# One 512-column matmul for the high and low part of the input, and two weight sums formed by accumulating DMAs

## The chip, the cores and the metric

One NeuronCore of a Trainium2 chip. The metric is device time of one launch in microseconds, the median of several runs. The engines are PE (matrix), DVE (vector), ACT (scalar), POOL and SP; SP and ACT start plain DMAs here, and POOL starts none in the kernel before.

## The reference

A decoder block over 512 positions of width 2048, all float32: an input projection, two kinds of mixer heads, an output projection, and then a gated feed-forward part, which the change touches:

```
h = rms_norm(x, norm2) * (1 + sc2) + sh2
gate, val = split(h @ w_up, 2)              # w_up: 2048 x 12288, two halves of 6144
gate = causal_dwconv(gate, ffn_conv_w, ffn_conv_b)     # three taps along the sequence
x = x + g2 * ((gelu(gate) * val) @ w_down)  # w_down: 6144 x 2048
out = rms_norm(x, norm_final)
```

`sh2, sc2, g2` come from `silu(c) @ w_ada`, a conditioning product of a vector and a large matrix.

## The kernel before

**Precision.** Every operand of a large matmul is kept as two tiles of a rounded matmul type: a high part (the value rounded) and a low part (what rounding left off). A product is three matmuls: high weights by high input, high weights by low input, low weights by high input. For weights, ACT rounds a raw block (`round_up`, L162) and DVE subtracts (`rest`, L167).

**Steps.** The work is a list of steps, each with one weight block of 128 x 1024 numbers and 24 matmuls. The main loop issues, for step j: what is put at j with half -1; the rounding of the weights of step j+2; the fetch of raw weights for j+5; what is put at j with half 0; the remainder of the weights of j+2; the first half of the matmuls; what is put with half 1; the second half. Each engine works through its own instructions in that order, so `put(j, fn, cost, half)` decides where a small piece of work stands in DVE's, ACT's, SP's or POOL's queue. Buffers come from pools with a fixed number per tag; a tile waits until the last user of its buffer is done.

**The up projection.** The first four columns of 128 features (steps UP0 to UP0+15) are plain: 512-column matmuls over 16 blocks of the input. For the other 44 columns, gate, value, the two halves of the positions and the two halves of the 2048 inputs make a 2 x 2 by 2 x 2 block product, which is done with seven products instead of eight (`P1` to `P7`, `product`, L859). For each product a step multiplies a sum of weight blocks by a sum of input blocks; 8 blocks of 128 inputs, 256 positions, three matmuls of 256 columns each (L875 to L877). Every product uses only the first half (`lower`) of a PSUM bank. The steps of a column go P1, then P4 and P3 of the column before, then P2, P6, P5, P7.

`combine` (L820) forms the four sums of input blocks (DVE), rounds them (ACT) and takes the remainders (DVE), one portion k of eight per plain step from UP0+8 on. `column` (L896) does the rest for a column: four weight blocks are loaded on SP (`split_load`), DVE forms four sums of them (t1 to t4), ACT copies P1, P6, P7 and P4 out of PSUM (`after_p1` and so on), DVE adds P2, P7 and P3 to those copies, then the convolution taps, gelu, the product of gate and value, and a store to DRAM (`act_kept`) on SP.

**The down projection** (steps from J1 on) loads these activations again (`act_load`, L1044), splits them (`act_split`, L1048) and multiplies by w_down with 512-column matmuls, in two halves of 24 activations, four groups of 12 steps each. After a group, `settle` (L978) adds the group's banks to the residual with a factor g2, whose 16 columns come from `g2_load` (1 MB of w_ada into one buffer) and `ada` (a product on DVE, L209), put at J1+4 to J1+35. There are six banks for groups, and a group takes four.

Of the kernel before, what the change touches and what calls it, by code (L numbers as in the profile page):

```python
# [50 lines left out]
def tile_block(ctx, tc, x_t, vec, w_ada, w_in, w_r, w_i, ws_t, w_out, w_up, w_us, w_dn, out):  # L51
# [144 lines left out]
    def ada_load(n, pl=mid):  # L196
        w = D + (2 if n // KT in (1, 4) else 1)
        loads[0] += 1
        front = pl is mid and early_open and loads[0] % 3 == 0
        if front:  # L200
            raw = sb("araw2", 1, (P, D + 2), pl=fore)
        else:
            raw = sb("araw", 2 if pl is mid else 1, (P, D + (2 if pl is mid else 32)), pl=pl)
        SY.dma_start(raw[:, :w], w_ada[n, :, :w])
        return n, raw[:, :w], w, front

# [613 lines left out]
    def combine(k):  # L820

        a, b = x2[k], x2[k + KT // 2]
        sh, shb = (mod(3 * KT + n) for n in (k, k + KT // 2))
        st = sb("rawb", 4, (P, 4, HS), pl=ffn)
        V.scalar_tensor_tensor(out=st[:, 1, :], in0=a[:, upper], scalar=shsum[:, k:k + 1], in1=b[:, upper],
                               op0=ADD, op1=ADD)
        V.scalar_tensor_tensor(out=st[:, 0, :], in0=st[:, 1, :], scalar=sh, in1=a[:, lower], op0=SUB, op1=SUB)
        V.tensor_tensor(out=st[:, 2, :], in0=a[:, upper], in1=a[:, lower], op=SUB)
        V.scalar_tensor_tensor(out=st[:, 3, :], in0=b[:, lower], scalar=shb, in1=st[:, 0, :], op0=ADD, op1=SUB)
        sums[k] = []  # L830
        for i in range(4):
            two = sb("sx", 8, (P, 2, HS), F32R, ffn) if k in (2, 3) else sb("xs", NXS, (P, 2, HS), F32R)
            A.copy(two[:, 0, :], st[:, i, :])
            sums[k].append(two)

        def rest():
            for i in range(4):
                V.tensor_tensor(out=sums[k][i][:, 1, :], in0=st[:, i, :], in1=sums[k][i][:, 0, :], op=SUB)
        return rest

    def combine_all():
        V.tensor_tensor(out=shsum, in0=mods[:, 3 * KT:3 * KT + KT // 2], in1=mods[:, 3 * KT + KT // 2:4 * KT], op=ADD)
# [16 lines left out]
    def product(f, p):  # L859
        j = len(steps)  # L860
        place[p, f] = j
        b = INTO[p]
        source[j] = lambda: of[f][p]

        def go(kk):
            if p in ("P1", "P2", "P5") and kk == 0:
                of[f][b] = bank()
            ps = of[f][b][:, lower]
            hi, lo = ws[j][kk]
            for k in range(4 * kk, 4 * kk + 4):  # L870
# [18 lines left out]
            product(n, p)  # L889

    def split_load(f, i, tag):
        t = sb("raw", 4, (P, 2, S)) if tag == "raw" else sb("rawb", 4, (P, 2, S), pl=ffn)
        SY.dma_start(t, w_us[f - PLAIN, i])
        return t

    def column(f):  # L896
        o = of[f]
        at_ = {p: place[p, f] for p in INTO}
        s = at_["P1"]

        def load(name, i, tag):
            o[name] = split_load(f, i, tag)

        put(s - 6, lambda: load("P1", 0, "raw"), 0.0, 1)
        put(s - 5, lambda: load("b12", 1, "raw"), 0.0, 1)
        put(s - 4, lambda: load("P3", 3, "rawb"), 0.0, 1)
        put(s - 3, lambda: load("P2", 2, "rawb"), 0.0, 1)

        def t1():
            V.tensor_tensor(out=o["P1"], in0=o["b12"], in1=o["P1"], op=SUB)  # L910
            o["P5"] = o["P1"]

        def t2():
            o["P6"] = sb("t2", 1, (P, 2, S), pl=ffn)
            V.tensor_tensor(out=o["P6"], in0=o["P3"], in1=o["P5"], op=SUB)

        def t3():
            V.tensor_tensor(out=o["b12"], in0=o["b12"], in1=o["P3"], op=SUB)
            o["P7"] = o["b12"]

        def t4():
            V.tensor_tensor(out=o["P2"], in0=o["P2"], in1=o["P6"], op=SUB)
# [6 lines left out]
        def half(tag):  # L929
            return sb(tag, 1, (P, HS), pl=ffn)  # L930

        def after_p1():
            o["c1"] = half("c1")
            A.copy(o["c1"], o["x"][:, lower])

        def after_p2():
            o["g"] = sb("fg", 2, pl=ffn)
            V.tensor_tensor(out=o["g"][:, lower], in0=o["z"][:, lower], in1=o["c1"], op=ADD)

        def after_p6():  # L940
            o["u2"] = half("u2")
            A.copy(o["u2"], o["x"][:, lower])

        def after_p7():
            u3 = half("u3")
            A.copy(u3, o["x"][:, lower])
            o["v"] = sb("fv", 2, pl=ffn)
            V.tensor_tensor(out=o["v"][:, upper], in0=o["y"][:, lower], in1=u3, op=ADD)

        def after_p4():  # L950
            A.copy(o["g"][:, upper], o["x"][:, lower])
# [3 lines left out]
        def after_p3():  # L955
            V.tensor_tensor(out=o["v"][:, lower], in0=o["y"][:, lower], in1=o["u2"], op=ADD)

        def times():
            V.tensor_tensor(out=o["fy"], in0=o["fy"], in1=o["v"], op=MUL)
# [7 lines left out]
        put(at_["P3"] + 2, lambda: tap(f, o["fy"], o["g"], 1))  # L967
# [23 lines left out]

    def weigh(n, apart=False):

        q = sb("yl", 3, pl=room2[0]) if n else xs()
        A.activation(q, x2[n], AF.Square)  # L995
        w = sb("yl", 3, pl=room2[0]) if apart else x2[n]
        V.tensor_scalar(out=w, in0=x2[n], scalar1=gfh[:, n:n + 1], scalar2=None, op0=MUL)
        x2[n] = w
        if n:
            V.tensor_tensor(out=total[0], in0=total[0], in1=q, op=ADD)  # L1000
        else:
            total[0] = q
# [37 lines left out]
                group_by_column(srcs, ks, act, down_tail, 2)  # L1040

    yls = {}

    def act_load(f):  # L1044
        yls[f] = sb("yl", 3, pl=room2[0] or ffn)
        SY.dma_start(yls[f], kept[f])

    def act_split(f):  # L1048
        y = yls.pop(f)
        two = pair() if f < 16 or 27 <= f < 43 else sb("dp", 11, (P, 2, S), F32R, room2[0])  # L1050
        A.copy(two[:, 0, :], y)
        V.tensor_tensor(out=two[:, 1, :], in0=y, in1=two[:, 0, :], op=SUB)
        act[f] = (two[:, 0, :], two[:, 1, :], two)

    def second_room():
        opened.pop().__exit__(None, None, None)
# [154 lines left out]
```

## Time and profile before

| | us |
|---|---|
| median of 3 runs | 2150.6 (2147.19 to 2150.71) |
| the profiled execution | 2149.32 |
| its span, first to last instruction | 2147.6 |
| mean granted clock of the matrix engine | 0.989 of 2.4 GHz |

The span is what the trace's times count from; 1.7 us of the execution lie around it. A timeline row is a start, a duration, the engine, the source line, the operation and its tiles; in brackets stand the idle time before it and what ended that. Durations of matmuls overlap, so starts are compared.

### The profile page before, as it was taken

Reading aid. Unit: us, or ns where it says so; the run is one execution under the profiler, and the core shown is the slowest. Engines: PE = TensorE matmul, PEld = TensorE weight load, DVE = VectorE, ACT = ScalarE, POOL = GpSimd, SP = SyncE. Lnnn points to the kernel's source line nnn. Section 1 sums busy time; section 2 is a strip of 40 time slices with the busy share of each in tenths; the row PEclk is TensorE's granted clock in tenths of the full one; section 3 lists DMA queues with packets and bytes.
Section 4 is the critical chain, followed back from the end, with each engine's and each line's share of the span. In section 5 each row is a group of like instructions: output and inputs, shape, how many; then the busy total and the mean of one; then the engine's idle time right before and its main releaser. Section 6 shows DMA issues by size and latency. Waiting matters only on the chain. (4 is left out here: it accounts for less than half of the span.)

```text
span 2147.6 us, 30757 instructions
## 1 busy us (share of the span) xinstructions
PE 2094.9 (98%) x12620; PEld 1861.4 (87%) x12620; DVE 1508.0 (70%) x1851; ACT 875.0 (41%) x1148; POOL 4.7 (0%) x12
## 2 busy tenths in 40 slices
PE   7999999999989999999999999999998999999996
PEld 4887778888768999999999999999997888888885
DVE  8999889787768777877877877877865444432333
ACT  5323775332234544544544444444452112222222
POOL 0000000000000000000000000000000000000000
PEclk8999999999999999999999999999999999999998
DMA  9876443679822333233233233233256555422222
GB/s 369 331 286 222 147 157 129 225 285 336 301 96 99 126 131 131 93 132 128 94 133 127 95 133 127 95 133 127 96 182 258 217 210 182 160 91 98 89 98 79
DMA packets 97069, 351.43 MB, mean 164 GB/s; under 512 B 12704, under 2 KB 12832, under 8 KB 84640
## 3 DMA queue, kind: packets, MB, share of 16 engines
q1 hardware_dynamic: 81520, 293.36, 38.3%
q10 hardware_dynamic: 15408, 56.11, 7.2%
q8 instruction: 99, 1.62, 0.3%
q14 instruction: 42, 0.34, 0.0%
HBM read 328.45 MB, written 20.97 MB: 163 GB/s over the span
## 5 line engine op out<-in xcount | busy, mean ns | idle before, releaser
L162 ACT CAST wh<-raw 128x1024 fp32r<-128x1024 f32 x340 | 356.9, 1050 | 694.4 <-PE mm L174 483.8
L167 DVE TENSOR_TENSOR wl<-raw,wh 128x1024 fp32r<-128x1024 f32 x340 | 416.0, 1224 | 238.4 <-ACT wh L162 235.8
L173 PE MATMUL mm<-hp,wh 128*128 128x512 f32 x1280 | 508.7, 397 | 15.2 <-DVE xs L979 5.8
L175 PE MATMUL mm<-hp,wl 128*128 128x512 f32 x1280 | 502.2, 392 | 3.1 <-DVE wl L167 3.1
L174 PE MATMUL mm<-hp,wh 128*128 128x512 f32 x1280 | 502.5, 393 | 0.8 <-DVE hp L234 0.8
L173 PEld LDWEIGHTS mm<-hp,wh 128*128 128x128 f32 x1280 | 242.7, 190 | 72.4 <-ACT hp L226 9.1
L877 PE MATMUL mm<-xs,wl 128*128 128x256 f32 x1056 | 299.1, 283 | 0.6 <-DVE wl L167 0.5
L875 PE MATMUL mm<-xs,wh 128*128 128x256 f32 x1056 | 298.9, 283 | 0.0
L876 PE MATMUL mm<-hp,wh 128*128 128x256 f32 x1056 | 298.9, 283 | 0.0
L877 PE MATMUL mm<-hp,wl 128*128 128x256 f32 x1056 | 298.8, 283 | 0.0
L875 PE MATMUL mm<-hp,wh 128*128 128x256 f32 x1056 | 298.8, 283 | 0.0
L876 PE MATMUL mm<-xs,wh 128*128 128x256 f32 x1056 | 298.8, 283 | 0.0
L175 PEld LDWEIGHTS mm<-hp,wl 128*128 128x128 f32 x1280 | 242.5, 189 | 55.1 <-DVE wl L167 4.4
L174 PEld LDWEIGHTS mm<-hp,wh 128*128 128x128 f32 x1280 | 242.5, 189 | 54.3 <-issue 2.4
L209 DVE SCALAR_TENSOR_TENSOR araw<-araw,crow 128x2050 f32<-128x2050 f32 (+1 forms) x96 | 219.8, 2291 | 44.0 <-DMA araw<-w_ada 44.0
L167 DVE TENSOR_TENSOR wl<-rawb,wh 128x1024 fp32r<-128x1024 f32 x132 | 161.7, 1225 | 76.7 <-ACT wh L162 76.7
L877 PEld LDWEIGHTS mm<-xs,wl 128*128 128x128 f32 x1056 | 202.7, 192 | 1.0 <-DVE wl L167 1.0
L875 PEld LDWEIGHTS mm<-hp,wh 128*128 128x128 f32 x1056 | 202.7, 192 | 0.0
L875 PEld LDWEIGHTS mm<-xs,wh 128*128 128x128 f32 x1056 | 202.7, 192 | 0.0
L876 PEld LDWEIGHTS mm<-hp,wh 128*128 128x128 f32 x1056 | 202.7, 192 | 0.0
L877 PEld LDWEIGHTS mm<-hp,wl 128*128 128x128 f32 x1056 | 202.7, 192 | 0.0
L876 PEld LDWEIGHTS mm<-xs,wh 128*128 128x128 f32 x1056 | 202.7, 192 | 0.0
(214 smaller groups left out, 2615.5 us busy)
## 6 DMA issues: line engine op xcount, KB each, us to landing
araw<-w_ada SPq DMA_DIRECT2D x64, 1024.5 KB, 5.9
raw<-w_dn SPq DMA_DIRECT2D x96, 512.0 KB, 3.4
raw<-w_us SPq DMA_DIRECT2D x88, 512.0 KB, 4.5
rawb<-w_us SPq DMA_DIRECT2D x88, 512.0 KB, 4.9
araw<-w_ada SPq DMA_DIRECT2D x32, 1025.0 KB, 7.2
raw<-w_in ACTq DMA_DIRECT2D x59, 512.0 KB, 4.0
raw<-w_out ACTq DMA_DIRECT2D x32, 512.0 KB, 6.1
act_kept<-fy SPq DMA_DIRECT2D x48, 256.0 KB, 2.2
```

Of the source, the lines that this page charges most:

```text
L162: A.copy(hi, raw)
L167: V.tensor_tensor(out=lo, in0=raw, in1=hi, op=SUB)
L173: PE.matmul(ps, w[0][:, cs], h[0], start=first, stop=False)
L174: PE.matmul(ps, w[0][:, cs], h[1], start=False, stop=False)
L175: return PE.matmul(ps, w[1][:, cs], h[0], start=False, stop=last)
L209: V.scalar_tensor_tensor(out=raw, in0=raw, scalar=1.0, in1=crow[:, :w], op0=MUL, op1=MUL, accum_out=mods[:, n:n + 1])
L875: PE.matmul(ps, hi[:, cs], m[:, 0, :], start=first, stop=False, skip_group_check=True)
L876: PE.matmul(ps, hi[:, cs], m[:, 1, :], start=False, stop=False, skip_group_check=True)
L877: PE.matmul(ps, lo[:, cs], m[:, 0, :], start=False, stop=last, skip_group_check=True)
```

## The change

The two matmuls with the high weights become one of 512 columns: the moving operand is the pair of the high and the low part, and the result goes into both halves of the bank. The matmul with the low weights still writes the first half alone.

```diff
-            ps = of[f][b][:, lower]
+            ps = of[f][b]
+            both = ps.rearrange("p (a b) -> p a b", a=2)
...
-                PE.matmul(ps, hi[:, cs], m[:, 0, :], start=first, stop=False, skip_group_check=True)
-                PE.matmul(ps, hi[:, cs], m[:, 1, :], start=False, stop=False, skip_group_check=True)
-                PE.matmul(ps, lo[:, cs], m[:, 0, :], start=False, stop=last, skip_group_check=True)
+                PE.matmul(both, hi[:, cs], m, start=first, stop=False, skip_group_check=True)
+                PE.matmul(ps[:, lower], lo[:, cs], m[:, 0, :], start=False, stop=last, skip_group_check=True)
```

The signs of the seven products are turned so that weight sums are additions. Sums t1 and t3 are no longer made on DVE: block 1 is loaded twice, and block 0 and block 3 are added to the two copies by DMAs that POOL starts.

```diff
-        put(s - 6, lambda: load("P1", 0, "raw"), 0.0, 1)
-        put(s - 5, lambda: load("b12", 1, "raw"), 0.0, 1)
-        put(s - 4, lambda: load("P3", 3, "rawb"), 0.0, 1)
+        def add(name, i):
+            G.dma_start(o[name], w_us[f - PLAIN, i], accum_op=ADD)
+
+        early_ = 6 if f == PLAIN else 7
+        put(s - early_, lambda: load("P5", 1, "raw"), 0.0, 1)
+        put(s - 6, lambda: load("P1", 0, "rawb"), 0.0, 1)
+        put(s - early_ + 2, lambda: add("P5", 0), 0.0, 1)
+        put(s - 5, lambda: load("P3", 3, "rawb"), 0.0, 1)
+        put(s - 4, lambda: load("P7", 1, "raw"), 0.0, 1)
+        put(s - 2, lambda: add("P7", 3), 0.0, 1)
         put(s - 3, lambda: load("P2", 2, "rawb"), 0.0, 1)
-
-        def t1():
-            V.tensor_tensor(out=o["P1"], in0=o["b12"], in1=o["P1"], op=SUB)
-            o["P5"] = o["P1"]
...
-        for i, t in enumerate((t1, t2, t3)):
-            put(at_["P6"] - 4 + i, t, 0.0, 1)
+        put(at_["P6"] - 3, t2, 0.0, 1)
```

What comes out of PSUM is twice as wide, and the two halves are added at the end: the gate before its taps, the value after them.

```diff
-            A.copy(o["c1"], o["x"][:, lower])
+            o["c1"] = copied("c1")
...
-            V.tensor_tensor(out=o["g"][:, lower], in0=o["z"][:, lower], in1=o["c1"], op=ADD)
+            o["gw"] = wide("gw")
+            V.tensor_tensor(out=o["gw"][:, :, lower], in0=two(o["z"]), in1=two(o["c1"]), op=ADD)
...
+        def gate():
+            o["g"] = sb("fg", 1, pl=ffn)
+            V.tensor_tensor(out=o["g"], in0=o["gw"][:, 0, :], in1=o["gw"][:, 1, :], op=ADD)
...
+        def value():
+            V.scalar_tensor_tensor(out=o["vw"][:, 0, :], in0=o["vw"][:, 0, :], scalar=-1.0, in1=o["vw"][:, 1, :],
+                                   op0=MUL, op1=SUB)
...
+        put(at_["P4"] + 2, gate)
+        put(at_["P3"] + 2, lambda: tap(f, o["fy"], o["g"], 1), 0.0, 1)
...
+        put(at_["P3"] + 3, value, 0.0, 1)
```

The portions of `combine` begin a step later, and the seventh and eighth share a step. The fourth input sum goes into the half of the plain input's tile that no product reads any more, and no longer into tiles of its own (`sx` is gone); the tag `rawb` has five buffers instead of four.

```diff
-            put(UP0 + 8 + k, lambda k=k, rests=rests: rests.append(combine(k)))
-            put(UP0 + 8 + k, lambda rests=rests: rests[0](), 0.0, 1)
+            j = UP0 + 9 + min(k, 6)
+            put(j, lambda k=k, rests=rests: rests.append(combine(k)))
+            put(j, lambda rests=rests: rests[0](), 0.0, 1)
...
-            two = sb("sx", 8, (P, 2, HS), F32R, ffn) if k in (2, 3) else sb("xs", NXS, (P, 2, HS), F32R)
-            A.copy(two[:, 0, :], st[:, i, :])
+            two = sb("xs", NXS, (P, 2, HS), F32R) if i < 3 else h2[k][2][:, :, upper]
+            A.activation(two[:, 0, :], st[:, i, :], AF.Copy, scale=-1.0 if i % 2 else 1.0)
```

In the down projection the first four activations go into other tiles, the loads of activations stand a step further ahead of their splits, with four buffers (`yl`) instead of three, and the conditioning loads and products are spread differently.

```diff
+    EARLY = 4
...
-        if f < 27:
+        if f < EARLY + 26:
             j = J1 + f // 2
-            first, then = (j - 3, j - 2) if f > 5 else (J1 + (-6, -6, -6, -3, -2, -1)[f], J1 + (-4, -3, -2, -1, 0, 0)[f])
+            first, then = (j - 4, j - 2) if f >= 8 else (J1 - 6, J1 - 2 + f // 2) if f < 4 else (J1 - 4 + f // 2, J1 - 2 + f // 2)
         else:
-            then = J1 + 37 + (f - 27) // 2
-            first = then - 1
+            then = J1 + 37 + (f - 26) // 2
+            first = then - 2
...
-        put(J1 + 4 + 2 * k, lambda k=k: g2_load(k))
-        put(J1 + 5 + 2 * k, lambda: ada(*g2_loaded.pop()))
+        j = J1 + (5 + 2 * k if k < 4 else 1 + 3 * k)
+        put(j, lambda k=k: g2_load(k))
+        put(j + (0 if k == 3 else 1), lambda: ada(*g2_loaded.pop()), 0.0, 1)
```

## Rows read from the trace of the kernel before

**Rows 1.** The page's engine table: busy us, share of the span, instructions.
```profile
PE 2094.9 (98%) x12620; PEld 1861.4 (87%) x12620; DVE 1508.0 (70%) x1851; ACT 875.0 (41%) x1148; POOL 4.7 (0%) x12
```

**Rows 2.** Windows, busy us (count): the seven products' stage.
```profile
core 0: us, PE busy (x) PEld busy (x) DVE busy (x) ACT busy (x) POOL busy (x), PEclk, DMA share, GB/s
697.00:1585.00 888.00, 887.43 (x7391) 886.89 (x7390) 701.76 (x750) 436.67 (x578) 0.00 (x0) 1.00 0.35 119
```

**Rows 3.** Waits in that stage, PE's: total us, times, longest.
```profile
PE mm L877 <- DVE wl L167: 0.5, 1, 0.5
```

**Rows 4.** Timeline, PE, matmuls of 256 columns (first and last of ten).
```profile
1299.82 0.28 PE L876 MATMUL mm<-hp,wh 128*128 128x256 f32 x1
...
1300.90 0.28 PE L876 MATMUL mm<-hp,wh 128*128 128x256 f32 x1
```

**Rows 5.** Timeline, PE, matmuls of 512 columns (first and last of thirteen).
```profile
400.06 0.39 PE L175 MATMUL mm<-hp,wl 128*128 128x512 f32 x1
...
402.78 0.39 PE L175 MATMUL mm<-hp,wl 128*128 128x512 f32 x1
```

**Rows 6.** Groups by line and shape: busy us, mean ns | idle before.
```profile
L162 ACT CAST wh<-raw 128x1024 fp32r<-128x1024 f32 x340 | 356.9, 1050 | 694.4 <-PE mm L174 483.8 <-PE mm L876 103.0 <-issue 57.0
L167 DVE TENSOR_TENSOR wl<-rawb,wh 128x1024 fp32r<-128x1024 f32 x132 | 161.7, 1225 | 76.7 <-ACT wh L162 76.7
L334 DVE TENSOR_TENSOR xs<-mm,xs 128x512 f32<-128x512 f32 x60 | 38.5, 685 | 2.2 <-PE mm L175 2.2
L1052 DVE TENSOR_TENSOR hp<-yl,hp 128x512 fp32r<-128x512 f32 x32 | 21.0, 689 | 44.8 <-ACT hp L1051 44.8
L938 DVE TENSOR_TENSOR fg<-mm,c 128x256 f32<-128x256 f32 x44 | 18.4, 419 | 0.0
L951 ACT COPY fg<-mm 128x256 f32<-128x256 f32 x44 | 16.4, 372 | 67.1 <-PE mm L877 67.1
L332 ACT COPY xs<-mm 128x512 f32<-128x512 f32 x20 | 11.2, 588 | 4.1 <-PE mm L175 2.9 <-PE mm L182 0.5
```

**Rows 7.** Timeline at the entry of that stage, DVE, and PE's one wait.
```profile
688.77 1.23 DVE L910 TENSOR_TENSOR raw<-raw,raw 128x1024 f32<-128x1024 f32 x1
...
691.26 0.48 DVE L825 SCALAR_TENSOR_TENSOR rawb<-xs,shsum,xs 128x256 f32<-128x256 f32 x1
...
695.24 1.42 DVE L838 TENSOR_TENSOR xs<-rawb,xs 128x256 fp32r<-128x256 f32 x4
696.58 1.53 DVE L806 SCALAR_TENSOR_TENSOR fy<-mm,vt,fy 128x511 f32<-128x511 f32 x2
...
702.76 1.23 DVE L167 TENSOR_TENSOR wl<-t,wh 128x1024 fp32r<-128x1024 f32 x1 [0.25 <-ACT wh L162]
704.04 0.39 PE L877 MATMUL mm<-xs,wl 128*128 128x256 f32 x1 [0.49 <-DVE wl L167]
```

**Rows 8.** Waits of SP's queue in that stage: total us, times, longest.
```profile
SPq L971 <- DVE fy L959: 617.0, 43, 14.6
```

**Rows 9.** The page's DMA issues: count, KB each, median us to landing.
```profile
raw<-w_us SPq DMA_DIRECT2D x88, 512.0 KB, 4.5
```

**Rows 10.** Timeline in the first group of the down projection.
```profile
1647.23 0.50 PE L175 MATMUL mm<-dp,wl 128*128 128x512 f32 x1 [0.74 <-DVE wl L167]
...
1648.11 0.38 SPq L1046 DMA_DIRECT2D yl<-act_kept  x1
...
1653.61 0.39 PE L175 MATMUL mm<-hp,wl 128*128 128x512 f32 x1
...
1655.69 2.29 DVE L209 SCALAR_TENSOR_TENSOR araw<-araw,crow 128x2049 f32<-128x2049 f32 x1
...
1659.04 2.72 DVE L979 SCALAR_TENSOR_TENSOR xs<-mm,mods,xs 128x512 f32<-128x512 f32 x4
1659.84 0.79 PE L173 MATMUL mm<-hp,wh 128*128 128x512 f32 x1 [5.85 <-DVE xs L979]
...
1663.28 0.39 PE L175 MATMUL mm<-hp,wl 128*128 128x512 f32 x1
```

**Rows 11.** The line of the conditioning loads (L204): time to landing.
```profile
DMA to landing us min/median/max: 4.8/6.3/11.4
```

More of the change, by code (lines that the diff above doesn't have):

```diff
@@ L202, in ada_load @@
         else:
-            raw = sb("araw", 2 if pl is mid else 1, (P, D + (2 if pl is mid else 32)), pl=pl)
+            raw = sb("araw", 2 if pl is mid else 1, (P, D + (2 if pl is mid else 64)), pl=pl)
         SY.dma_start(raw[:, :w], w_ada[n, :, :w])
@@ L837, in rest @@
             for i in range(4):
-                V.tensor_tensor(out=sums[k][i][:, 1, :], in0=st[:, i, :], in1=sums[k][i][:, 0, :], op=SUB)
+                lo, hi = sums[k][i][:, 1, :], sums[k][i][:, 0, :]
+                if i % 2:
+                    V.scalar_tensor_tensor(out=lo, in0=st[:, i, :], scalar=-1.0, in1=hi.bitcast(F32), op0=MUL, op1=SUB)
+                else:
+                    V.tensor_tensor(out=lo, in0=st[:, i, :], in1=hi, op=SUB)
         return rest
     def combine_all():
-        V.tensor_tensor(out=shsum, in0=mods[:, 3 * KT:3 * KT + KT // 2], in1=mods[:, 3 * KT + KT // 2:4 * KT], op=ADD)
+        V.tensor_tensor(out=shsum, in0=mods[:, 3 * KT:3 * KT + KT // 2], in1=mods[:, 3 * KT + KT // 2:4 * KT], op=SUB)
         for k in range(KT // 2):
             rests = []
-            put(UP0 + 8 + k, lambda k=k, rests=rests: rests.append(combine(k)))
-            put(UP0 + 8 + k, lambda rests=rests: rests[0](), 0.0, 1)
+            j = UP0 + 9 + min(k, 6)
+            put(j, lambda k=k, rests=rests: rests.append(combine(k)))
+            put(j, lambda rests=rests: rests[0](), 0.0, 1)
     put(UP0 + 7, combine_all)
@@ L891, in split_load @@
     def split_load(f, i, tag):
-        t = sb("raw", 4, (P, 2, S)) if tag == "raw" else sb("rawb", 4, (P, 2, S), pl=ffn)
+        t = sb("raw", 4, (P, 2, S)) if tag == "raw" else sb("rawb", 5, (P, 2, S), pl=ffn)
         SY.dma_start(t, w_us[f - PLAIN, i])
@@ L927, in column, with copied, two, wide @@
         put(max(at_["P6"] - 1, at_["P2"] - 2), t4, 0.0, 1)
-        def half(tag):
-            return sb(tag, 1, (P, HS), pl=ffn)
+        def copied(tag):
+            t = sb(tag, 1, pl=ffn)
+            A.copy(t, o["x"])
+            return t
+        def two(t):
+            return t.rearrange("p (a b) -> p a b", a=2)
+        def wide(tag):
+            return sb(tag, 1 + (tag == "vw"), (P, 2, S), pl=ffn)
         def after_p1():
-            o["c1"] = half("c1")
-            A.copy(o["c1"], o["x"][:, lower])
+            o["c1"] = copied("c1")
@@ L936, in after_p2 @@
         def after_p2():
-            o["g"] = sb("fg", 2, pl=ffn)
-            V.tensor_tensor(out=o["g"][:, lower], in0=o["z"][:, lower], in1=o["c1"], op=ADD)
+            o["gw"] = wide("gw")
+            V.tensor_tensor(out=o["gw"][:, :, lower], in0=two(o["z"]), in1=two(o["c1"]), op=ADD)
         def after_p6():
-            o["u2"] = half("u2")
-            A.copy(o["u2"], o["x"][:, lower])
+            o["u2"] = copied("u2")
         def after_p7():
-            u3 = half("u3")
-            A.copy(u3, o["x"][:, lower])
@@ L947, in after_p7, with after_p3 @@
-            o["v"] = sb("fv", 2, pl=ffn)
-            V.tensor_tensor(out=o["v"][:, upper], in0=o["y"][:, lower], in1=u3, op=ADD)
+            u3 = copied("u3")
+            o["vw"] = wide("vw")
+            V.tensor_tensor(out=o["vw"][:, :, upper], in0=two(o["y"]), in1=two(u3), op=ADD)
         def after_p4():
-            A.copy(o["g"][:, upper], o["x"][:, lower])
+            A.copy(o["gw"][:, :, upper], two(o["x"]))
+        def after_p3():
+            V.tensor_tensor(out=o["vw"][:, :, lower], in0=two(o["y"]), in1=two(o["u2"]), op=ADD)
@@ L958, in times @@
         def times():
-            V.tensor_tensor(out=o["fy"], in0=o["fy"], in1=o["v"], op=MUL)
+            V.tensor_tensor(out=o["fy"], in0=o["fy"], in1=o["vw"][:, 0, :], op=MUL)
         put(at_["P1"] + 1, after_p1, 0.0, -1)
@@ L992, in weigh @@
     def weigh(n, apart=False):
-        q = sb("yl", 3, pl=room2[0]) if n else xs()
+        q = sb("yl", 4, pl=room2[0]) if n else xs()
         A.activation(q, x2[n], AF.Square)
-        w = sb("yl", 3, pl=room2[0]) if apart else x2[n]
+        w = sb("yl", 4, pl=room2[0]) if apart else x2[n]
         V.tensor_scalar(out=w, in0=x2[n], scalar1=gfh[:, n:n + 1], scalar2=None, op0=MUL)
@@ L1042, in tile_block @@
     yls = {}
+    EARLY = 4
     def act_load(f):
[L1045 removed]
+        yls[f] = sb("yl", 4, pl=room2[0] or ffn)
         SY.dma_start(yls[f], kept[f])
@@ L1049, in act_split @@
         y = yls.pop(f)
[L1050 to L1053, printed above, removed]
+        if f < EARLY:
+            hi, lo = (sb("xs", NXS, dt=F32R) for _ in range(2))
+        else:
+            two = pair() if f < EARLY + 16 or EARLY + 26 <= f < EARLY + 42 else sb("dp", 10, (P, 2, S), F32R, room2[0])
+            hi, lo = two[:, 0, :], two[:, 1, :]
+        A.copy(hi, y)
+        V.tensor_tensor(out=lo, in0=y, in1=hi, op=SUB)
+        act[f] = (hi, lo)
     def second_room():
```

18 lines of the change are left out of this document (6 added, 12 removed).

## The prediction

> **What bounds the kernel now.** I read the page's engine table first: the matmul engine (PE) is busy 98% of the span, which leaves some 50 us without matmuls [rows 1]. A busy share says nothing of how fast the matmuls follow each other, so next come the windows by stage [rows 2]. The change lies in the long stretch from 697 to 1585 us, where w_up is multiplied in seven products for each of 44 columns of 128 features. There PE and its weight loads are busy without a break at a granted clock of 1.00, that is 2.4 GHz, VectorE (DVE) 79%, ScalarE (ACT) 49%, and the DMA engines 35%. The list of waits has 0.5 us of PE waiting for DVE in the whole stretch [rows 3]. So this stage is set by the distance from one matmul's start to the next, and the timeline gives that distance. With 256 columns ten starts lie 9 x 0.120 us apart (1.08 us) [rows 4]. With 512 columns, in an earlier stage with the same types, thirteen starts span 2.72 us, 0.2267 us each [rows 5]. The durations printed beside them (0.28, 0.39) are pipelined and can't be added. Check: 44 x 7 x 24 = 7392 matmuls x 0.120 = 887.0 us, and the stage is 888.3 us long (697.2 to 1585.5).
>
> **The matmuls.** For each block k the kernel issues three matmuls of 256 columns: high weights by high input, high weights by low input, low weights by high input; 3 x 0.120 = 0.360 us. After the change the first two are one matmul of 512 columns, which writes two halves of a bank, and the third stays: 0.2267 + 0.120 = 0.3467 us. The difference, 0.0133 us, is what each matmul costs here beyond its columns (256 at 2.4 GHz are 0.1067, 512 are 0.2133). There are 44 x 7 x 8 = 2464 such triples, so the stage loses 2464 x 0.0133 = **32.9 us**. The step of 24 matmuls falls from 2.88 to 2.77 us, the column of seven from 20.2 to 19.4. The trace shows no 512-column matmul whose input is two runs of 256, as it is in four of the seven products (P1, P2, P4, P3; the other three read a tile in one piece). Bounds for that: 0.2267, the row of the same width, and 0.240, two narrow ones; I take the first, since the narrow matmuls already read such runs at full pace.
>
> **Work that grows beside it.** What the low input contributes now lands in the upper half of a bank and has to be added later. Per column, ACT gets four copies out of PSUM of 512 instead of 256 columns, each +0.22 us (588 against 372 ns) [rows 6]. DVE loses two sums of weight blocks (1.22 each) [rows 7], and gets three PSUM sums of double width, each +0.27 (685 against 419), one gate sum and one value sum of the same width: 15.95 us per column now (701.8/44) becomes 15.95 - 2.44 + 0.80 + 1.38 = 15.7, to 16.6 if successive starts overlap less; 81 to 86% of 19.4. The heaviest step is the one under P2: P3's sum 0.69, gate sum 0.69, weight remainder 1.22, P2's weight sum 1.22, 3.8 against 2.77. The remainder that it delays is needed two steps later, that is 5.5 us after the step began; the cast before it (1.05) and the queue ahead end it 1.9 us or more before its use in every step when I lay out the column with these durations. Cost: zero, hidden under PE. If that margin were used up, each microsecond per column would cost 44 us.
>
> **The accumulating DMAs.** Two of the four sums now come from a third kind of transfer: a block is loaded, then a second block is added to it on its way, issued from POOL. POOL does nothing else in this stage. Per column there are five loads and two adds instead of four loads. SP runs far ahead: it stands 14 us per column before the store of the activation [rows 8], and issues the next column's loads as soon as that goes, some seven steps before the first sum that reads them. POOL's add waits for its load (4.5 us to landing [rows 9]); behind it is only the next add. So latency is covered by 10 us and more, and throughput decides. The engines' share of 0.35 of 888 us is 7.06 us per column for four blocks and a half-sized store, 1.57 us a block [rows 2]. Five loads and the store then take 8.6 us, and 10.8 of 19.4 us are left: each add may take 5.4 us, 3.4 times a load, before transfers set the pace. No row has an add. From below it costs a load, 1.57; from above I know only the landing time of a whole load, 4.5, were it all engine time; both fit. I take 3.1, two passes over the data. The Trainium skill, Collectives: The Full Stack, section The bandwidth ceiling, says that an add in the DMA path needs two source reads where a copy needs one, which by these rows would be 3.1 us; no run here shows it yet, and the sum stays as it is.
>
> **Entry of the stage.** Preparing the seven products' inputs is moved one step later, and two of eight portions now share the last step before the stage. Now the last such step runs without a gap on DVE: the weight sum 688.77, then the portion from 691.26 to 696.58, then the activation taps, then the remainder at 702.76, for which PE waits 0.49 us at 704.04 [rows 7]. After the change the same step holds a second portion (1.65 us of sums, 1.5 of remainders by starts), less the weight sum that goes (1.15): everything behind is 2.2 us later, and P6 starts 0.2 us earlier: the wait becomes some 3.1 us, **+2.7 us**. Bounds: 0, if the earlier portions leave more room, and +5, a full portion and a cast in sequence.
>
> **Exit of the stage.** Twelve steps into the last matmul group there is the longest wait of PE, 5.8 us: a start at 1653.61, the next at 1659.84, and then eight intervals (to 1663.28) at about 0.43, so at 1.2 GHz [rows 10]. That is 6.0 us lost in the gap, 1.6 by the lower clock, and 0.7 by another wait at 1647: 8.3. The chain behind it: an activation load leaves SP at 1648.11 behind a 1 MB conditioning load, its split holds DVE, the conditioning product (2.29 us) starts at 1655.69, and only then the first bank is emptied at 1659.04. After the change activations are loaded a step earlier with a fourth buffer, so that part goes. What is late next is the fourth conditioning load: its only buffer comes free when the third product ends in step 10: 0.1 + cast 1.05 + a split's cast 0.6 + two splits 1.3 + remainder 1.15 + product 2.3 = 6.5 us after that step began [rows 6, 10], or 1.1 into step 11 (a step is 24 x 0.2267 = 5.44). A median 6.3 us later the load lands [rows 11], 2.0 into step 12; the product and one settling (0.75) end 5.1 into it, while PE runs out of free banks after six matmuls, at 1.4. Wait 3.7, clock about 1: 4.7 against 8.3, **-3.6 us**. By the fastest landing (4.8) the wait is 2.2, a gain of 6.1; by the slowest (11.4) 8.8 and 1.6 of clock, a loss of 2.1.
>
> **Sum.** Profiled execution 2149.3 us (its span 2147.6 and 1.7 around it): - 32.9 + 2.7 - 3.6 = 2115.5. The median of the runs shown is 1.3 above that execution, within their spread of 3.5, so I say 2116. The likeliest case's own range is 2108 (exit at its best, no entry loss) to 2125 (entry +5, exit +2.1, spread).
>
> **Rivals.**
> 1. Only part of the 0.0133 us is saved, because an input in two runs costs again what two matmuls cost. For: nothing shows the form. Against: narrow runs stream at full pace now. If only the three one-piece products gain, 44 x 24 x 0.0133 = 14.1 us: 2149.3 - 14.1 - 0.9 = 2134.
> 2. The cost per matmul is not what separates the two widths. By rows 4 and 5 it is 0.0133; if it were a fifth of that (some 0.0025) and the rest belonged to columns, the stage would gain 2464 x 0.0025 = 6.2 us: 2142. The rows speak against it: both widths fit columns plus 0.0133. The Trainium skill, TensorE: Matmul & The Clock Gate, section Wait - 56ns, not 53.3ns?, gives about 2.5 ns per warm matmul, which is where such a case would come from; the trace here differs, 13.3 ns at both widths, and the measurement decides.
> 3. Slower: the adds. At 3.4 times a load the DMA engines fill the shortened column; at 3.7 times (5.8 us) they eat the whole gain; at five times (7.85 us) a column takes 8.6 + 15.7 = 24.3 us, 4.1 more than now: 44 x 4.1 - 0.9 = 180 us slower, 2328. PE would wait at P6 in each column for the weight sum. For: the price is unseen, and each add reads memory and SBUF and writes again. Against: 10.8 us of free engine time per column.
> 4. DVE becomes the bound, at 86% and with POOL writing transfer lists beside it. It would take 2.8 us more per column to begin, and 0.8 us beyond that to cancel the 32.9; nothing in the stage is near that. Around 2149.
>
> **Chances.** Main case 0.70, first rival 0.08, second 0.03, third 0.14, fourth 0.05. A measurement of this kernel can tell 0.2%, 4.3 us. Faster: the main case and the first two rivals with part of the fourth, 0.83; same 0.03; slower 0.14. The range 2108 to 2136 holds the main case and the first rival.
>
> **What would show it.** In the stage: by windows, a stretch of about 857 us instead of 888 with PE still busy throughout; a 512-column start followed 0.227 us later by a 256-column one and 0.120 later by the next. Per column DVE about 16 us, ACT about 11. DMA share some 0.75, an add's landing under 8 us, and no PE wait on weights after the first column. At the entry one wait of about 3 us at P6; at the exit one of 2 to 4 us on the settling, with no split late before it. Wrong would be: an interval above 0.23 after the wide matmul, PE waiting for weight remainders in every column, or a DMA share near 1.

## The result and the profile after

| | before | after |
|---|---|---|
| median, run side by side, us | 2150.5 | 2116.0 |
| the profiled execution | 2149.32 | 2116.15 |
| its span | 2147.6 | 2114.4 |

The ratio is 0.986, with an interval of 0.982 to 0.990; 2116 had been predicted. The kernel after, run once more, took 2116.9 us beside 2150.2 (0.984, 0.980 to 0.988). Single executions of it lie between 2109 and 2130 us in these two comparisons, those of the kernel before between 2147 and 2160.

The page's engine table of the kernel after answers to [rows 1] (busy us, share of the span, instructions), and behind it stand, from the same page, the queue of accumulating DMAs (packets, MB, share of 16 engines' span) and two rows of the DMA issues (count, KB each, median us to landing), plain loads and adds.

```profile
PE 2059.5 (97%) x10156; PEld 1729.2 (82%) x10156; DVE 1494.1 (71%) x1851; ACT 914.2 (43%) x1148; POOL 80.6 (4%) x100
...
q0 software_dynamic: 12672, 46.14, 11.4%
...
raw<-w_us SPq DMA_DIRECT2D x88, 512.0 KB, 5.5
raw<-w_us POOLq DMA_DIRECT2D x88, 512.0 KB, 7.3
```

The 2464 matmuls that were to go are gone (12620 - 10156). The share of PE hardly moves, so this table can't say where the time went. The windows view does, with the stretch of the seven products as in [rows 2]:

```profile
core 0: us, PE busy (x) PEld busy (x) DVE busy (x) ACT busy (x) POOL busy (x), PEclk, DMA share, GB/s
697.00:1555.00 858.00, 855.90 (x4922) 753.82 (x4921) 690.71 (x755) 474.78 (x579) 73.00 (x85) 1.00 0.69 200
```

The windows are set to the stage, which takes 858.5 us where it took 888.2. DVE has 15.7 us of work per column (690.71/44), ACT 10.8, and the transfers take 0.69 of the DMA engines. The timeline in it shows the new rhythm, to be held against [rows 4, 5]; columns are start, duration, engine, line, operation.

```profile
999.53 0.39 PE L881 MATMUL mm<-hp,wh 128*128 128x512 f32 x1
999.76 0.28 PE L882 MATMUL mm<-hp,wl 128*128 128x256 f32 x1
999.88 0.39 PE L881 MATMUL mm<-hp,wh 128*128 128x512 f32 x1
...
1000.92 0.39 PE L881 MATMUL mm<-hp,wh 128*128 128x512 f32 x1
```

Four pairs of a wide (512-column) and a narrow (256-column) matmul start within 1.39 us (999.53 to 1000.92): 0.347 us a pair, the 0.2267 + 0.120 of the prediction. The moving operand `hp` is the one in two runs; pairs with `xs`, in one piece, start as far apart (346.7 ns on average for both, behind the entry).

The waits of PE (total us, times, longest): one at the exit of the stage, two at its entry.

```profile
PE mm L173 <- DVE xs L997: 5.3, 1, 5.3
...
PE mm L881 <- ACT c L934: 1.8, 1, 1.8
...
PE mm L882 <- DVE wl L167: 0.3, 1, 0.3
```

Cut at the first matmul of the seven products, at the first of the down projection and at the first one on the last tile `yl` near the end, the two profiled executions differ so:

| stretch | before | after | difference |
|---|---|---|---|
| up to the seven products | 697.3 | 700.2 | +2.9 |
| the seven products | 888.2 | 858.5 | -29.7 |
| the down projection | 544.3 | 538.3 | -6.0 |
| the end | 17.8 | 17.5 | -0.3 |

The sum before rounding is -33.2, the difference of the spans.

### The profile page after: what moved, and what is told of

Same layout as the page of the kernel before. It is cut to its first block, busy times and chain, and to the rows that moved or that the text cites. A ratio compares the mean times of both kernels' runs of the same rounds, so it can differ in the third digit from the quotient of the medians.

```text
span 2114.4 us, 26281 instructions
## 1 busy us (share of the span) xinstructions
PE 2059.5 (97%) x10156; PEld 1729.2 (82%) x10156; DVE 1494.1 (71%) x1851; ACT 914.2 (43%) x1148; POOL 80.6 (4%) x100
## 5 line engine op out<-in xcount | busy, mean ns | idle before, releaser
L167 DVE TENSOR_TENSOR wl<-raw,wh 128x1024 fp32r<-128x1024 f32 x296 | 361.7, 1222 | 265.7 <-ACT wh L162 261.5
L173 PE MATMUL mm<-hp,wh 128*128 128x512 f32 x1280 | 508.1, 397 | 13.0 <-DVE xs L382 6.0
L174 PE MATMUL mm<-hp,wh 128*128 128x512 f32 x1280 | 502.1, 392 | 0.5 <-DVE hp L234 0.5
L881 PE MATMUL mm<-hp,wh 128*128 128x512 f32 x1408 | 490.2, 391 | 0.0
L882 PE MATMUL mm<-hp,wl 128*128 128x256 f32 x1408 | 394.2, 280 | 0.0
L881 PE MATMUL mm<-xs,wh 128*128 128x512 f32 x1056 | 369.7, 392 | 1.8 <-ACT c L934 1.8
L881 PEld LDWEIGHTS mm<-hp,wh 128*128 128x128 f32 x1408 | 263.3, 187 | 57.8
L173 PEld LDWEIGHTS mm<-hp,wh 128*128 128x128 f32 x1280 | 242.4, 189 | 69.6 <-ACT hp L226 8.7
L175 PEld LDWEIGHTS mm<-hp,wl 128*128 128x128 f32 x1280 | 242.2, 189 | 54.8 <-DVE wl L167 4.2
L174 PEld LDWEIGHTS mm<-hp,wh 128*128 128x128 f32 x1280 | 242.3, 189 | 53.7 <-issue 2.4
L882 PEld LDWEIGHTS mm<-hp,wl 128*128 128x128 f32 x1408 | 266.1, 189 | 0.0
L881 PEld LDWEIGHTS mm<-xs,wh 128*128 128x128 f32 x1056 | 198.3, 188 | 45.7 <-ACT c L934 2.1
L162 ACT CAST wh<-rawb 128x1024 fp32r<-128x1024 f32 x176 | 185.8, 1056 | 12.5 <-issue 7.5
L910 POOL DMA_DIRECT2D raw<-w_us x88 | 75.7, 860 | 1267.8 <-DMA raw<-w_us 666.6
L167 DVE TENSOR_TENSOR wl<-t,wh 128x1024 fp32r<-128x1024 f32 x44 | 53.9, 1225 | 50.6 <-ACT wh L162 50.6
```

Source lines behind the costliest of these rows:

```text
L162: A.copy(hi, raw)
L167: V.tensor_tensor(out=lo, in0=raw, in1=hi, op=SUB)
L173: PE.matmul(ps, w[0][:, cs], h[0], start=first, stop=False)
L174: PE.matmul(ps, w[0][:, cs], h[1], start=False, stop=False)
L175: return PE.matmul(ps, w[1][:, cs], h[0], start=False, stop=last)
L881: PE.matmul(both, hi[:, cs], m, start=first, stop=False, skip_group_check=True)
```

## Experiments

Each is the kernel after with the edit shown, but for the second of "The address", which starts from the kernel before, and for `e8_both` and `e10_both_two`, which put edits shown earlier together. Stages are from one profiled execution, times are medians.

### Is it the matmul count? `e1_two_narrow`

```diff
-                PE.matmul(both, hi[:, cs], m, start=first, stop=False, skip_group_check=True)
+                PE.matmul(ps[:, lower], hi[:, cs], m[:, 0, :], start=first, stop=False, skip_group_check=True)
+                PE.matmul(ps[:, upper], hi[:, cs], m[:, 1, :], start=False, stop=False, skip_group_check=True)
```

> The merge alone undone: the wide matmul is two of 256 columns again, the second into the other half of the bank; everything else stays as changed. Theory A (the gain is the 13.3 ns that each matmul costs beyond its columns): 2464 triples x 0.0133 = 32.9 us longer, 2149 us, three starts 0.120 us apart, no new wait. Theory B (part of the gain comes from lighter DVE or from transfers): clearly less than 32.9 comes back. A narrow matmul into the upper half that costs more than 0.120 would show as over 33.

2145.7 us (ratio 0.997, 0.996 to 0.999), 28.8 more than the kernel after beside it (`again`), and the stage is 891.0 us, 32.5 longer than there (858.5). Its timeline:

```profile
999.63 0.28 PE L883 MATMUL mm<-hp,wl 128*128 128x256 f32 x1
...
1001.19 0.28 PE L881 MATMUL mm<-hp,wh 128*128 128x256 f32 x1
```

These are fourteen starts, 13 x 0.120 us. A triple takes 360.0 ns and a pair 346.7, so the 2464 matmuls fewer are worth 13.3 ns each, 32.8 us, with all other parts of the change in place; the entry of the stage is 0.3 us cheaper with the triples. The two spans differ by less than the stage, since this profiled execution reached the stage 6.8 us earlier (694.4 against 701.2), in code that is the same in both.

### Do the adds by DMA pay, and what do they cost? `e2_dve_sums`, `e5_adds6`

```diff
-            G.dma_start(o[name], w_us[f - PLAIN, i], accum_op=ADD)
+            V.tensor_tensor(out=o[name], in0=o[name], in1=o[i], op=ADD)
...
-        put(s - early_ + 2, lambda: add("P5", 0), 0.0, 1)
+        put(s - 1, lambda: add("P5", "P1"), 0.0, 1)
...
-        put(s - 2, lambda: add("P7", 3), 0.0, 1)
+        put(at_["P6"] - 2, lambda: add("P7", "P3"), 0.0, 1)
```

> The two accumulating DMAs undone: block 1 is still loaded twice, but block 0 and block 3 are added to it by DVE (two sums of 1.22 us per column more), and POOL starts nothing. Theory A (the adds only unload DVE, which has room): DVE 15.4 + 2.3 = 17.7 of 19.5 us per column, the stage stays 858 us, the kernel as the changed one within 0.2%. Theory B (without the adds DVE is the bound, and the merge alone would not have paid in full): PE waits for weight remainders in every column, the stage 870 us or more. In both the DMA share of the stage falls from 0.69 to about 0.41, so if the executions with a slower pace of the matmul pairs (353 instead of 347 ns) come from the denser transfers, none is seen here.

2116.8 us (0.986, 0.981 to 0.990), like the kernel after; the stage is 859.7 us. Windows view:

```profile
697.00:1555.00 858.00, 854.64 (x4917) 746.64 (x4916) 780.77 (x841) 468.23 (x575) 0.00 (x0) 1.00 0.41 148
```

DVE has 2.0 us more per column (780.77 against 690.71 over 44), is 91% busy, and PE's waits for it in the whole stage are one of 0.3 us, at the entry. The adds by DMA buy no time here; the DMA share of 0.41 beside 0.69 is their price. The other way, with four more of them per column:

```diff
+        put(s - 3, lambda: more(2), 0.0, 1)
...
+        put(s - 1, lambda: add("P5", 0), 0.0, 1)
+        put(s, lambda: more(1), 0.0, 1)
+        put(s, lambda: add("P7", 3), 0.0, 1)
...
```

> The kernel after with four accumulating DMAs more per column: block 0 and block 3 are added to their sums twice, so these two weight sums differ from the reference's, and two adds go into a tile that nothing reads. Theory A (an add takes 2.74 us of all 16 DMA engines, by its queue's share in the kernel after): a column needs 13.5 + 4 x 2.74 = 24.4 us of transfers, more than its 19.5 us of matmuls, so the stage becomes 44 x 24.4 = 1075 us, the time some 2330, and PE waits for weight sums. Theory B (adds are cheap when more of them are under way, or their queue's share is mostly waiting): the DMA share rises to about 1 and the time stays within 20 us of 2116.

One execution, 2265.9 us, 150 more than the kernel after; the stage is 1008.8 us, 22.9 a column. Windows view, PE's waits and one of DVE's, landing times:

```profile
697.00:1706.00 1009.00, 921.69 (x4930) 777.88 (x4929) 691.94 (x753) 464.66 (x577) 220.95 (x256) 0.96 1.03 260
```

```profile
PE mm L881 <- ACT wh L162: 35.2, 18, 4.7
PE mm L881 <- ACT u L946: 25.8, 24, 2.7
PE mm L882 <- DVE wl L167: 24.2, 53, 0.8
```

```profile
DVE t L935 <- DMA raw<-w_us: 125.9, 38, 7.7
```

```profile
raw<-w_us POOLq DMA_DIRECT2D x176, 512.0 KB, 8.9
rawb<-w_us SPq DMA_DIRECT2D x132, 512.0 KB, 14.7
```

The DMA share is 1.03 (packets overlap), loads land after 14.7 us and not 5.6, DVE waits 125.9 us for blocks to land before it can form its sum (`t`), and PE waits on weights: transfers now set the pace, as theory A has it, though its 24.4 us a column and 2330 us were too much. Transfers take 0.69 x 858 / 44 = 13.5 us of all engines per column in the kernel after. From the two windows an add takes (22.9 x 1.03 - 13.5) / 4 = 2.5 us of all engines, and by its queue in the kernel after 0.114 x 2114.4 / 88 = 2.7: 1.6 to 1.7 of a load's 1.57.

### The address of the down projection's input. `e3_pad32`, `e7_before_pad64`

The first hunk of the diff lengthens a tile by 32 floats more. The tiles behind it in SBUF, the on-chip memory of the operands, move with it by 128 bytes, `dp` among them (the split activations). Undone in the kernel after, and done alone in the kernel before:

```diff
-            raw = sb("araw", 2 if pl is mid else 1, (P, D + (2 if pl is mid else 64)), pl=pl)
+            raw = sb("araw", 2 if pl is mid else 1, (P, D + (2 if pl is mid else 32)), pl=pl)
```

> Only the padding of the buffer of the conditioning loads is set back from 64 to 32 numbers, which moves the dp tiles (the activations' tiles of the down projection) by 128 bytes. Theory A (the address of dp against that of the weights sets its pace): matmuls with dp as moving operand 0.2332 us apart as in the kernel before, instead of 0.2266; 384 to 768 of them per type of operand, some 4 to 5 us longer in all, 2120 to 2121, hp and xs unchanged. Theory B (the pace hung on something else, as the amount of transfers): no change, 0.2266.

```diff
-            raw = sb("araw", 2 if pl is mid else 1, (P, D + (2 if pl is mid else 32)), pl=pl)
+            raw = sb("araw", 2 if pl is mid else 1, (P, D + (2 if pl is mid else 64)), pl=pl)
```

> The kernel before, with the one number of the first hunk alone: the conditioning row's tile is 64 floats longer than the data and not 32, which shifts the tiles that are allocated after it, those of the down projection's input dp among them, by 128 bytes. Theory A (a matmul of 512 columns starts every 226.7 ns, not 233.2, once the moving operand dp lies at an address of the same remainder by 256 as the weights): dp pace 226.7, down projection 4 us shorter and more at its exit stop or not, time 2145 to 2147 against about 2150.5; Theory B (the pace of dp belongs to other parts of the change): 233.2 and 2150.

The groups by line from 1700 to 2100 us, in the down projection, in the kernel before and in the kernel before with the longer tile (mean ns of one behind the bar):

```profile
L173 PE MATMUL mm<-dp,wh 128*128 128x512 f32 x204 | 80.6, 395 | 0.0
```

```profile
L173 PE MATMUL mm<-dp,wh 128*128 128x512 f32 x204 | 79.4, 389 | 0.0
```

The starts tell the pace. Sixteen starts in the kernel before, then seventeen in the changed one:

```profile
1979.78 0.39 PE L173 MATMUL mm<-dp,wh 128*128 128x512 f32 x1
...
1983.27 0.40 PE L173 MATMUL mm<-dp,wh 128*128 128x512 f32 x1
```

```profile
1979.65 0.39 PE L173 MATMUL mm<-dp,wh 128*128 128x512 f32 x1
...
1983.28 0.39 PE L174 MATMUL mm<-dp,wh 128*128 128x512 f32 x1
```

That is 3.49/15 = 0.233 us against 3.63/16 = 0.227. The one number takes the kernel before from 2152.4 to 2147.5 us (0.998, 0.997 to 0.999): 768 matmuls x 6.4 ns = 4.9. (Its profiled down projection is only 3.3 us shorter, since PE's two waits there came out at 6.1 and 1.4 us where they were 5.8 and 0.7.) In the kernel after without it the pace is 0.233 again and the down projection 6.2 us longer, of which 2.3 are a longer wait at the exit; its median is 2126.4 (0.988, 0.984 to 0.992), over executions of 2119, 2120, 2132 and 2133, for which the next group of experiments has a likely reason. By the addresses allocated in the built programs (the traces hold none) `dp` starts at a multiple of 256 bytes in the slow kernels and 128 bytes past one in the fast ones; the weights and `hp` are 128 past one in all. Whether it is the multiple itself or the distance from the weights that counts was not tested.

### The two stops, and the two paces. `e4_exit`, `e6_entry`, `e8_both`, `e9_two_by_two`, `e10_both_two`

PE's waits at the exit and the entry of the stage looked like 5 and 2 us to be had. The exit, by loading the first four conditioning blocks a step earlier:

```diff
-        j = J1 + (5 + 2 * k if k < 4 else 1 + 3 * k)
+        j = J1 + (4 + 2 * k if k < 4 else 1 + 3 * k)
...
-        put(j + (0 if k == 3 else 1), lambda: ada(*g2_loaded.pop()), 0.0, 1)
+        put(j + 1, lambda: ada(*g2_loaded.pop()), 0.0, 1)
```

> The first four conditioning loads of the down projection are put one step earlier (steps 4, 6, 8, 10), their products with them; nothing else differs. Theory A (the stop at step 12 is the fourth load, which leaves late because its one buffer comes free late): the stop goes or falls below 1.5 us, and with it 5.7 us of gap less 0.2 and 1.6 of lower clock, some 6 to 7 us: 2109 to 2110. Theory B (the load is slow because transfers are dense there, whenever it leaves): it stays above 4 us.

2118.8 us (0.983, 0.978 to 0.988), with executions from 2106 to 2126. The wait is gone from the profile and the down projection is 531.4 us, 7 less. But the stage before it takes 873.2 us in that execution, with pairs 353 ns apart all through it. The entry, by moving the activations of the last plain columns behind P6's remainder (`activation` cut in three pieces and put at later steps):

```diff
-            for e in range(2):
-                activation(2 * g + e, ps[e], ps[2 + e])
+            if g == 0:
...
+            for e, j in ((0, UP0 + 16), (1, UP0 + 18)):
+                for part, (d, fn) in enumerate(activation_parts(2 + e, ps[e], ps[2 + e])):
+                    put(j + (d if e else 0), fn, 0.0, 1)
```

> The activations of the last two plain columns, which stand ahead of P6's weight remainder in DVE's and ACT's queues at the entry of the stage, are put behind it: one in the same step, one spread over the three steps from UP0+18 on. Theory A (the entry wait is DVE's and ACT's queue): the waits at P6 (1.8 for the copy of P1 and 0.3 for the remainder, 2.6 by starts) fall below 0.5, the stage is some 2 us shorter, 856. Theory B (the input portions themselves are late): the waits stay.

2124.4 us (0.987, 0.985 to 0.990), where 856 us for the stage and a gain had been expected: some 8 above the medians of the kernel after (not run beside it, and the intervals overlap), though PE does not wait at the entry any more. Its timeline has the reason:

```profile
999.48 0.40 PE L905 MATMUL mm<-xs,wh 128*128 128x512 f32 x1
999.72 0.28 PE L906 MATMUL mm<-xs,wl 128*128 128x256 f32 x1
999.84 0.40 PE L905 MATMUL mm<-xs,wh 128*128 128x512 f32 x1
...
1001.25 0.40 PE L905 MATMUL mm<-xs,wh 128*128 128x512 f32 x1
```

Five pairs take 1.77 us, 0.354 each, and the stage 870.6. Both edits together:

> The earlier conditioning loads (7.3 us of the down projection, seen in its trace) and the entry order in one kernel. Theory A: 7 and 2 us add up, some 9 us under the changed kernel at the same pace of the matmul pairs, 2106 to 2108, and 2121 to 2123 in an execution whose pairs are 353 ns apart. Theory B (what one saves comes back as another wait): 2110 or more at the fast pace.

2119.7 us (0.985, 0.983 to 0.987): no wait at either end, 870.6 us for the stage again. So the same pairs run at 346.7 or at 353.3 ns, and 6.6 ns x 2464 are 16 us. That is about the spread of the kernel after, but none of its long executions was profiled.

The traces show where the pace changes. Every profile with this alternation begins the stage at the longer one; in the kernel after, the fifteen pairs ahead of the entry's stop take 5.29 us, 0.353 each:

```profile
700.21 0.39 PE L881 MATMUL mm<-hp,wh 128*128 128x512 f32 x1
...
705.50 0.40 PE L881 MATMUL mm<-hp,wh 128*128 128x512 f32 x1
```

Behind that stop PE's granted clock falls to 0.50 for some 2.5 us (that is 1.2 GHz; pairs are 0.64 us apart), and from its rise to the end of the stage the pairs are 346.7 ns apart. The profiles of `again`, `e2_dve_sums` and `e3_pad32` show the same. `e4_exit` has the same stop, but there the clock stays at 1.00, and the thirteen pairs behind it take 4.59 us, 0.353 each as ahead of it. The window of the kernel after, then the window and the timeline of `e4_exit`:

```profile
709.70:712.20 2.50, 2.50 (x10) 2.11 (x10) 2.50 (x4) 0.00 (x0) 0.00 (x0) 0.50 0.96 357
```

```profile
705.00:712.00 7.00, 4.90 (x27) 3.91 (x26) 5.99 (x6) 5.18 (x7) 0.00 (x0) 1.00 0.64 242
```

```profile
707.00 0.50 PE L881 MATMUL mm<-xs,wh 128*128 128x512 f32 x1 [1.83 <-ACT c L934]
...
708.35 0.40 PE L881 MATMUL mm<-xs,wh 128*128 128x512 f32 x1
...
712.94 0.40 PE L881 MATMUL mm<-xs,wh 128*128 128x512 f32 x1
```

In `e6_entry` and `e8_both`, without a stop, the pace and the clock stay as they begin. Next the order was changed, in the kernel after to wide, wide, narrow, narrow:

```diff
-            for k in range(4 * kk, 4 * kk + 4):
+            for k0 in (4 * kk, 4 * kk + 2):
+                for k in (k0, k0 + 1):
...
+                    PE.matmul(both, hi[:, cs], MOVING[p](k), start=first, stop=False, skip_group_check=True)
+                for k in (k0, k0 + 1):
...
+                    PE.matmul(ps[:, lower], lo[:, cs], MOVING[p](k)[:, 0, :], start=False, stop=last, skip_group_check=True)
```

> Only the order of the matmuls in the stage is changed: two wide ones, then their two narrow ones, in place of wide, narrow, wide, narrow. Theory A (the 353 ns per pair that one execution showed in place of 347 is a rhythm into which the alternation falls, since each narrow matmul must hide a weight load of its own length): the pace is 346.7 per pair in every execution, and the times lie within 6 us of each other. Theory B (the slower pace comes from outside the order, as from addresses or transfers): some executions are again 13 to 16 us longer than others. In neither is the fast pace better than 346.7, the sum of 226.7 and 120.

2118.0 us (0.984, 0.981 to 0.986), from 2115.7 to 2124.3: the pace is 348.3 ns a pair, but the stops are still there, with 7.6 us at the exit in the profiled execution, so alone the order gains nothing on the kernel after. And that order in the kernel of both edits:

> Both stops of PE are taken away (conditioning loads one step earlier; the activations of the last plain columns moved behind P6's remainder), and the matmuls of a step go wide, wide, narrow, narrow, not wide, narrow, wide, narrow. With the old order the kernel without stops had pairs 353.3 ns apart and took 2119.66. Theory A (the longer pace belongs to the strict alternation of a wide and a narrow matmul when PE never stops): pairs 346.7 to 348 apart, stage of the seven products 855 to 859, time 2104 to 2109. Theory B (it comes with running without a stop, in any order): pairs about 353, stage about 870, time 2118 to 2122.

2106.3 us beside 2152.4 (0.979, 0.977 to 0.982), with executions of 2105.8, 2106.0, 2106.6 and 2109.9. Windows view of the stage and of the exit:

```profile
697.00:1555.00 858.00, 858.00 (x4922) 748.43 (x4921) 690.62 (x755) 474.34 (x581) 73.15 (x85) 1.00 0.69 200
1555.00:1660.00 105.00, 104.98 (x470) 86.82 (x469) 64.53 (x75) 39.25 (x54) 0.00 (x0) 1.00 0.71 251
```

PE is idle for 0.02 us of these 963, the stage is 858.3 us (348.3 ns a pair) and the down projection 531.3. Theory A of that run holds: against `e8_both` only the order differs, and it takes the pairs from 353.3 to 348.3 ns. Its median is the lowest of all, 10 us below those of the kernel after, of whose eight executions none was below 2108.8; one of its own four took 2109.9, and the two were not run side by side.

### The kernel after once more, `again`

> The changed kernel as it is, on this chip, for comparison with the runs beside it. Every theory: within 0.2% of 2116 us, the products' stage 858 us long, a stop of 5 to 6 us twelve steps into the down projection, and matmuls with dp as moving operand 0.2267 us apart. Whether the 2.9 us that the profiled execution lost ahead of the stage, in the output projection, comes again is open: if it is scatter, the stage begins anywhere between 697 and 700 us.

2116.9 us (2108.8 to 2129.3); the profiled execution has the stage at 858.5 us and `dp` at 227 ns, as the first.

## Why the prediction came out

**The matmuls: right.** Predicted -32.9, measured 32.8 by the intervals of `e1_two_narrow` (32.5 for its whole stage), and the pair's two intervals add up to the predicted 0.3467 us from the entry on. That they can also add up to 0.3533 no step of the prediction has. The first rival (an input in two runs costs again) falls: `hp` and `xs` pairs keep the same pace. So does the second, a smaller cost per matmul. The Trainium skill, TensorE: Matmul & The Clock Gate, section Wait - 56ns, not 53.3ns?, has 2.5 ns per warm matmul; the runs here have 13.3, five times as much, and with 2.5 the change would have been worth 6 us.

**The growing work: right.** DVE 15.7 us per column, the low end of the predicted 15.7 to 16.6, ACT 10.8; PE waits for neither after the first column. `e2_dve_sums` shows how large the cover is: 2.0 us more of DVE per column cost nothing. This speaks against the fourth rival too.

**The adds: right, the price too high.** Taken at 3.1 us of engine time, measured 2.5 to 2.7; landing 7.3 us, predicted under 8; share 0.69, predicted some 0.75. The third rival, slower by 180 us, needed an add of five loads; it is 1.6 to 1.7. Its mechanism is real, as `e5_adds6` shows. The Trainium skill's two source reads for an add (Collectives: The Full Stack, section The bandwidth ceiling) put it nearer than the bounds from the rows did, and still above the measurement.

**The entry: about right in size, but the engine was another and the clock was left out.** Predicted +2.7, from DVE's queue ahead of P6's remainder (its terms, 1.65 + 1.5 - 1.15, add up to 2.0 and not to the 2.2 that it used). The timeline at the entry:

```profile
706.40 0.69 DVE L814 TENSOR_TENSOR fy<-mm,fy 128x512 f32<-128x512 f32 x1 [0.76 <-ACT fy L813]
707.21 0.57 ACT L934 COPY c<-mm 128x512 f32<-128x512 f32 x1
707.33 1.23 DVE L167 TENSOR_TENSOR wl<-t,wh 128x1024 fp32r<-128x1024 f32 x1 [0.24 <-ACT wh L162]
707.84 0.50 PE L881 MATMUL mm<-xs,wh 128*128 128x512 f32 x1 [1.83 <-ACT c L934]
708.61 0.39 PE L882 MATMUL mm<-xs,wl 128*128 128x256 f32 x1 [0.28 <-DVE wl L167]
```

PE stops first for ACT's copy out of PSUM (1.83 us) and then 0.28 for the remainder. By starts it loses 2.6 us, against 0.85 before: +1.8. ACT's copy is late behind the same activations as DVE's remainder, and goes away with them in `e6_entry`; I had followed DVE's queue alone. To this comes a term that the prediction had at the exit and not here: the lower clock behind the stop, shown above, costs 1.6 us, where the clock before stayed at 1.00. The entry is +3.4 in all. A wait of 0.3 us near the end of the stage is gone, and with the first fifteen pairs at the longer pace (0.1 us) the stage comes to -32.8 + 3.4 - 0.3 + 0.1, some -29.7.

**The exit: the step was right, its size was not.** Predicted -3.6. The conditioning load left SP close to the predicted point (1619.43, 6.3 us into step 10, predicted 6.5), but the landing was longer:

```profile
1619.43 0.33 SPq L204 DMA_DIRECT2D araw<-w_ada  x1
...
1627.83 2.29 DVE L209 SCALAR_TENSOR_TENSOR araw<-araw,crow 128x2049 f32<-128x2049 f32 x1 [5.19 <-DMA araw<-w_ada]
1630.05 2.06 DVE L997 SCALAR_TENSOR_TENSOR xs<-mm,mods,xs 128x512 f32<-128x512 f32 x3
```

8.4 us and not the median of 6.3 [rows 11]. So PE waits 5.3 us where I had 3.7, and the lower clock behind it costs 1.8 where I had about 1:

```profile
1625.16 0.39 PE L175 MATMUL mm<-xs,wl 128*128 128x512 f32 x1
1630.85 0.80 PE L173 MATMUL mm<-xs,wh 128*128 128x512 f32 x1 [5.30 <-DVE xs L997]
1631.44 0.63 PE L174 MATMUL mm<-xs,wh 128*128 128x512 f32 x1
1631.87 0.63 PE L175 MATMUL mm<-xs,wl 128*128 128x512 f32 x1
```

```profile
1632.00:1633.00 1.00, 1.00 (x4) 0.81 (x3) 1.00 (x3) 0.00 (x0) 0.00 (x0) 0.50 0.00 0
```

The intervals of 0.43 us after the wait are those of 1.2 GHz, as in [rows 10]; the windows view, its last line above, has a granted clock of 0.50. The gap is 0.55 us shorter than before, the slow tail 0.2 longer, and the wait of 0.74 at 1647 is gone: -1.1 in all. `e4_exit` shows that this stop, with its tail, was worth 7 us.

**What no step named.** The hunk on the padding stands in the diff, and I gave it no line. It is most of the down projection's -6.0: 768 matmuls on `dp` before at 233.2 ns, after 576 on `dp` and 192 on other tiles at 227, -4.9. With the exit's -1.1 this is the stretch. Against it stand the +2.9 ahead of the stage, of which the longer waits of the output projection (6.0 against 2.7 us on the residual, L382) are the larger part, in code that the change leaves alone. This stretch ends at 694.4 to 702.0 us in the kernels of this study, so I count it as scatter; that was not tested.

So 2116 is right for its main term, -32.9, and by luck in the small ones: an exit 2.5 us worse than predicted, an entry 0.7 worse and 2.9 us ahead of the stage, against 4.9 from an address and 0.7 from the last wait of the stage and the end. There is luck in the pace too: the stop at the entry, predicted as a cost alone, is where the profiled execution went over to the shorter one. The range of 2108 to 2136 covered the two paces without my knowing of them: `e4_exit`, with the same entry, has a stage 14.7 us longer, which would make some 2131 of the kernel after, and two of its eight executions took 2129 and 2130.

**Left open.** Why PE settles in one pace or the other, and why its clock fell behind the entry's stop in the kernel after and not in `e4_exit`. A passage at the lower clock is not the whole of it: in `e5_adds6`, with many stops, 18 such passages are followed by pairs at 346.7 ns in eleven cases and at 353 in seven. Nor is one needed: the pace changes there across stops at full clock too. Denser transfers are not needed for the longer pace, if the one execution of `e2_dve_sums` at 2139.8 was of that kind, which its profile (of another execution) does not show.

## What to carry to other kernels

Where PE is busy all through, count matmuls and not only columns, and take the cost of one from starts at two widths in the trace itself. After a change to PE's sequence read its start intervals in more than one execution: a kernel can lose at its pace what it gained at a stop, and an order of wide, wide, narrow, narrow kept to 348.3 ns a pair in both kernels that had it, where strict alternation took 346.7 or 353.3. And give every hunk a line in the sum, a changed padding too.

## What the runs showed of the hardware

- A 512-column matmul started every 226.8 ns with its moving operand 128 bytes past a multiple of 256, like the weights, and every 233.2 ns with it on such a multiple. One number in an allocation moved 4.9 us.
- The same alternation of wide and narrow matmuls ran at 346.7 or 353.3 ns a pair for 845 us and more on end, at a granted clock of 1.00 in both. In four profiles the pace went from the longer to the shorter one across a passage of some 2.5 us at a granted clock of 0.50, and stayed there. Three narrow ones kept to 3 x 120.0 in all three profiles that have them.
- An accumulating DMA into SBUF took 2.5 to 2.7 us of engine time for 512 KB where a load took 1.57, landed after 7.3 us where loads of the same tiles took 5.5, and kept POOL busy 0.86 us.
